# Sums of quarters kept in DRAM, and the last chunk of a down projection by seven products

## Chip, cores and metric

The kernel runs on one core of a Trainium2 chip. The metric is the device time of one execution in microseconds. The median of three runs of the kernel before is 2237.82 us (2236.54 to 2239.23).

## What is computed

Two decoder layers over 1024 tokens of width 1024. Layer 0 mixes tokens by a convolution module, layer 1 by sliding-window attention. In both, the mixer is followed by a layer norm, a squared-ReLU MLP with 4096 inner features, another layer norm, and a gated embedding. The change touches the MLP:

```python
def sq_relu_mlp(x, w_up, w_down):
    return jnp.square(jax.nn.relu(x @ w_up)) @ w_down
...
x = layer_norm(DEEPNORM_ALPHA * x + sq_relu_mlp(x, mlp_w_up[i], mlp_w_down[i]),
               mlp_ln_g[i], mlp_ln_b[i])
x = x + (p[i] @ ple_w_proj[i]) * jax.nn.sigmoid(x @ ple_w_gate[i])
```

## The kernel before

All matmuls are of float32 data, each operand split in a high part and a low part of the type fp32r. One product of a 128x128 block with a 128x512 block is three matmuls (`mm3`): high by high, high by low, low by high. Splitting is a cast on ScalarE (ACT) for the high part and a subtraction on VectorE (DVE) for the low one. A subtraction recorded for `nc.either` goes to DVE or to GpSimd (POOL).

The program is first recorded as a list of operations, each with a priority (its place in the list, plus an offset inside `later`). `Recorder.schedule` then runs through the list with a table of estimated costs and writes out a fixed order for each engine: at each moment it takes the ready operation with the lowest priority. Buffers are slots under tags ("t" has five, "z" four, "g" four, "wh" and "wl" five each, "raw" two, "zz" one, "bo" two), given out in the order of the requests and taken back when the last user ends. The eight PSUM banks are slots too, under "ps" and "tr" (transposes); `move` hands a slot from one tag to another. All DMAs are issued by SyncE, in one queue. Since a recorder writes every instruction, all of them carry one line in the profile (L433); tiles are told apart by their tag.

**Up products** (`mlp`). The 4096 inner features are 32 blocks of 128. The first four blocks in layer 0 (six in layer 1) and the last two are multiplied block by block (`up`: per block and half of the tokens, eight products over the width, 24 matmuls). The others go in pairs of blocks: a pair and the two halves of the tokens are a 2x2 problem, done with seven products of quarters (84 matmuls) instead of eight; sums of weight quarters (`pair_units`) and of token quarters (`token_forms`) are made on DVE. `square` applies relu and squares the result, and stores it at once in DRAM. `hid[i][c, j, h]` holds, for chunk c (four inner blocks), the blocks of parity j and the tokens of half h: a quarter of 128x1024, in two stores of 256 KB.

**Down products** (`down_seven`, `down_last`). The inner features are eight chunks of 512. A chunk is again a 2x2 problem: A is quarters of inner activations (half of the tokens by half of the chunk), B is quarters of `w_down`. `down_seven` does chunk 0 alone and chunks 1 to 6 two at a time (`DOWN`), by seven products. It loads quarters of A, and DVE makes the sums s1 to s4 of A and t1 to t4 of B. `form` splits each operand into tiles of xTh and xTl (eight of them in turn), and in the first chunk into tiles under `hid_tags`. `product` does the matmuls for four token tiles, into four banks, and `add_to` adds each bank to the residual tiles `self.x[t][q]` on DVE. Two groups of four banks are used: `one` for the products that share a1.b1, and `two`.

`down_last` does chunk 7 without sums: 8 products, run token tile by token tile, eight tiles of 24 matmuls. As soon as a token tile is complete, `layer_norm(t)` runs for it: statistics (DVE, with a power on POOL), scaling (ACT), gain (DVE), bias (`either`), then eight transposes on TensorE (PE) and their splits into xTh and xTl.

**The gate** (`ple`) follows at once: x @ w_gate for four token tiles at a time, first tiles 0 to 3, then 4 to 7, 24 matmuls a tile, from xTh and xTl. Its four weight units go through `prep` (load to "raw", cast on ACT, subtraction on `either`); in `down_last` the four units of `w_down` hold four of the five "wh" and "wl" slots until the last tile.

Of the kernel before, what the change touches and what calls it, by code (L numbers as in the profile page):

```python
# [15 lines left out]
P = 128  # L16
# [4 lines left out]
HT = 512  # L21
# [444 lines left out]
class Emit:  # L466
# [379 lines left out]
                    if cc == 1:  # L846
                        self.layer_norm(t, gb, self.mid[i])

    def square(self, i, f, h, src, tag="t"):
# [5 lines left out]
        nc.vector.scalar_tensor_tensor(out=sq, in0=src, scalar=0.0, in1=r, op0=ALU.max, op1=ALU.mult)  # L855
        o = f % 4 // 2 * HT
        nc.sync.dma_start(self.hid[i][f // 4, f % 2, h][:, o : o + HT], sq)

    def up(self, i, f, h, u):
# [5 lines left out]
        self.square(i, f, h, ps)  # L865

    def pair_units(self, i, f):

# [84 lines left out]
    def mlp(self, i):  # L953
# [9 lines left out]
        us = ws.get(4)  # L963
        for h in range(2):
            for f in first[:4]:
                self.up(i, f, h, us[f])
        ws.done(4)
        for f in first[4:]:
# [31 lines left out]
        for f in pairs:  # L1000
            w = ws.get(1)[0]
            p = prod(w, 0, plain[0, 0])
            c11 = copy(p)
            p2 = prod(w, 1, plain[1, 0])
            ws.done(1)
            w12 = ws.get(1)[0]
            prod(w12, 0, T[2], p)
            c21 = copy(p)
            self.square(i, f, 0, plus(c11, p2), "z")
# [5 lines left out]
            self.square(i, f + 1, 1, plus(c22, r), "z")  # L1015
            w = ws.get(1)[0]
            prod(w34, 1, plain[1, 1], p)
            self.square(i, f, 1, p, "z")
            prod(w, 0, T[4], r)
            ws.done(2)  # L1020
            self.square(i, f + 1, 0, plus(c21, r), "z")
        for f in last:
            u = ws.get(1)[0]
            for h in range(2):
                self.up(i, f, h, u)
            ws.done(1)

        self.x = []
        for t in range(NT):
# [3 lines left out]
        for k in range(3):  # L1033
            nc.move("tr", "ps")
        for n, cs in enumerate(DOWN):
            self.down_seven(i, cs, self.hid_tags if n == 0 else "")
        for k in range(3):
            nc.move("ps", "tr")
        gb = self.load_row("g", d["mlp_g"][i : i + 1]), self.load_row("g", d["mlp_b"][i : i + 1])
        self.down_last(i, NC - 1, gb)  # L1040

    def add_to(self, t, q, ps):

# [29 lines left out]
        self.nc.sync.dma_start(v, ap)  # L1073
        return v

    def down_seven(self, i, cs, tags):

        nc, d = self.nc, self.d
        sub, add = ALU.subtract, ALU.add
        n = len(cs)

        def A(tag, h, j):
            return [self.quarter(tag, self.hid[i][c, j, h]) for c in cs]

        def B(tag, j, q):
            return [self.quarter(tag, d["w_down"][i, c, j, q]) for c in cs]  # L1090

        def halves(tag, other):
            if tags:
# [12 lines left out]

        ftags = list(tags)

        def product(a, b, to, bank=None):
            f = [[self.form(v, ftags.pop(0) if ftags else None) for v in p] for p in zip(a, b)]  # L1110
# [15 lines left out]
        a11, b11 = A("wh", 0, 0), B("wl", 0, 0)  # L1126
        if tags:
            residual(0, 0)
        one = product(a11, b11, [(0, 0)])
        if tags:  # L1130
            m = [o for o in nc.ops if o.eng == "tensor"]
            residual(1, 1, m[-24 * n])
            residual(1, 0, m[-12 * n])
            residual(0, 1, m[-1])
        product(A("raw", 0, 1), B("wl", 1, 0), [(0, 0)])
        a21, b12 = A("wh", 1, 0), B("wl", 0, 1)
# [4 lines left out]
        s3 = tt(halves("z", 0), a11, a21, sub)  # L1141
        t3 = tt(halves("g", 1), b22, b12, sub)
        two = product(s3, t3, [(1, 1)])
        a22 = A("raw", 1, 1)
        s1 = tt(a21, a21, a22, add)
        s2 = tt(a11, s1, a11, sub)
# [4 lines left out]
        a12 = A("wh", 0, 1)  # L1151
        s4 = tt(a12, a12, s2, sub)
        product(s4, b22, [(0, 1)], one)
        a22, b21 = A("raw", 1, 1), B("wl", 1, 0)
        t4 = tt(b21, b21, t2, sub)
        product(a22, t4, [(1, 0)], two)

    def down_last(self, i, c, gb):

        nc, ws = self.nc, self.ws  # L1160
        ws.add(*[self.d["w_down"][i, c, j, q] for j in range(2) for q in range(2)])
        hid = {}
        for h in range(2):
            for j in range(2):
                for k in range(2):
                    raw = self.sb("t")
                    nc.sync.dma_start(raw, self.hid[i][c, j, h][:, k * HT : (k + 1) * HT])
                    hid[2 * k + j, h] = self.pair(self.hid_tags[h], F32R)
                    self.split(raw, *hid[2 * k + j, h])
        us = ws.get(4)  # L1170
        for t in range(NT):
            pss = [self.ps() for q in range(2)]
            o = t % 4 * P
            for b in range(4):
                hh, hl = hid[b, t // 4]
                for q in range(2):
                    wh, wl = us[b % 2 * 2 + q]
                    cs = slice(b // 2 * HT, (b // 2 + 1) * HT)
                    self.mm3(pss[q], [(hh[:, o : o + P], hl[:, o : o + P], wh[:, cs], wl[:, cs])], b == 0, b == 3)
            for q in range(2):  # L1180
                self.add_to(t, q, pss[q])
            self.layer_norm(t, gb)
        ws.done(4)

    def ple(self, i):
        nc, d, ws = self.nc, self.d, self.ws
# [40 lines left out]
    def attention(self):  # L1227
# [67 lines left out]
                    pend = p, n, gl, dict(vd), dst  # L1295
            ws.done(4)
        self.values(*pend)
        for a, b in (("ps", "sc"), ("ps", "sc"), ("ps", "pv")):
            nc.move(b, a)

        self.x = []
# [88 lines left out]
    def program(self):  # L1390
# [13 lines left out]
        for i in range(2):  # L1404
            for t in range(NT):
                nc.slots(f"mid{i}_{t}", [f"mid{i}_{t}"])
            for c in range(8):
                for k in range(4):
                    nc.slots(f"hid{i}_{c}_{k}", [f"hid{i}_{c}_{k}"])
        self.mid = [[nc.tile(f"mid{i}_{t}", (P, D), F32, "DRAM") for t in range(NT)] for i in range(2)]  # L1410
        self.hid = [
            {(c, k // 2, k % 2): nc.tile(f"hid{i}_{c}_{k}", (P, 1024), F32, "DRAM") for c in range(8) for k in range(4)}
            for i in range(2)
        ]
        self.ws = Stream(self)
# [103 lines left out]
```

## Time and profile before

| | |
|---|---|
| median of three runs | 2237.82 us |
| time of the profiled execution | 2238.38 us |
| its span | 2236.6 us |
| granted TensorE clock, mean | 0.998 |
| layer 0: first down chunk starts | 736.6 us |
| layer 0: last chunk of the down products | 1003.1 us |
| layer 0: gate products start | 1052.5 us |
| layer 1: waits of PE behind the last chunk | 2144.7 to 2155.1 us |

The profiled execution is one run of its own; its span runs from its first to its last instruction, and 1.8 us lie around it. "Busy" counts an instruction from start to end, and instructions of one engine overlap a little, so a sum of durations is more than the time they take one behind the other. PEld is the loading of weights into the array, which runs beside PE. A wait is put down to the engine that released it last.

### The profile page before, as it was taken

To read this page: it belongs to the slowest core of one execution; us is meant where nothing else is said; L and a number is where in the kernel's file an instruction comes from. 1 tells how busy PE (TensorE), PEld (TensorE's weight loads), DVE (VectorE), ACT (ScalarE), POOL (GpSimd) and SP (SyncE) were. 2 spreads that over 40 slices of the span, in tenths; PEclk is the share of its full clock that TensorE was granted. 3 is DMA by queue.
4 is the path that set the end of the run, shared out by engine and by line. 5 is a ranking of instruction groups with operands and counts; after the bars stand their busy time and mean duration, and the time that the engine had idled before them with its cause. 6 is when DMAs were issued, how large, how long until landed. Compare 5 with 4: busy or idle time off the path is not lost.

```text
span 2236.6 us, 28918 instructions
## 1 busy us (share of the span) xinstructions
PE 2196.3 (98%) x10412; PEld 1811.7 (81%) x10412; DVE 1601.4 (72%) x2596; ACT 927.1 (41%) x1709; POOL 361.2 (16%) x497
## 2 busy tenths in 40 slices
PE   8999999999999999999999999999999999999999
PEld 6888878788888888887778878777888888888877
DVE  6666586965555999978354888579565579889663
ACT  4333353544443333433245878333344433344231
POOL 2333362200000000005001555131000000000230
PEclk9999999999999999999999999999999999999999
DMA  7444642523336753530431011332333493444222
GB/s 222 109 111 98 170 132 82 194 85 113 113 113 199 254 168 127 170 118 19 132 99 38 21 38 39 106 106 81 103 110 113 119 318 129 158 160 132 66 85 99
DMA packets 128656, 271.38 MB, mean 121 GB/s; under 512 B 14081, under 2 KB 41857, under 8 KB 128513
## 3 DMA queue, kind: packets, MB, share of 16 engines
q1 hardware_dynamic: 128512, 269.54, 38.1%
q8 instruction: 82, 1.34, 0.3%
q14 instruction: 62, 0.50, 0.1%
HBM read 202.38 MB, written 67.11 MB: 120 GB/s over the span
## 4 chain that ended last, share of the span: by engine, by line
PE 87%; DVE 6%; POOL 2%; issue 1%; ACT 1%; DMA 1%; SPq 0%; POOLq 0%; DVEq 0%; ACTq 0%
PE ps L433 70%; PE tr L433 17%; DVE z L433 2%; DVE sm L433 1%; POOL sm L433 1%; DVE xTl L433 1%; DVE wl L433 1%; POOL B L433 1%; DVE E L433 1%; DMA raw<-in_w_in_dram 1%; ACT z L433 0%; DVE B L433 0%; DVE A L433 0%; SPq L433 0%; POOL wl L433 0%
## 5 line engine op out<-in xcount | busy, mean ns | idle before, releaser
L433 PE MATMUL ps<-xTh,wh 128*128 128x512 f32 x668 | 261.4, 394 | 4.7 <-ACT xTh L433 4.7
L433 PE MATMUL ps<-xTl,wh 128*128 128x512 f32 x668 | 263.1, 394 | 2.8 <-DVE xTl L433 2.8
L433 PE MATMUL ps<-xTh,wl 128*128 128x512 f32 x668 | 261.4, 391 | 0.0
L433 DVE TENSOR_TENSOR wl<-raw,wh 128x1024 fp32r<-128x1024 f32 (+2 forms) x130 | 145.8, 1124 | 133.2 <-ACT wh L433 132.2
L433 ACT CAST wh<-raw 128x1024 fp32r<-128x1024 f32 (+2 forms) x146 | 137.6, 943 | 230.7 <-PE ps L433 116.3
L433 PE MATMUL ps<-wh,xTh 128*128 128x512 f32 x572 | 230.2, 402 | 1.6 <-DVE xTh L433 1.5
L433 PE MATMUL ps<-wl,xTh 128*128 128x512 f32 x572 | 230.5, 403 | 0.0
L433 PE MATMUL ps<-wh,xTl 128*128 128x512 f32 x572 | 229.4, 402 | 0.1
L433 POOL TENSOR_TENSOR wl<-raw,wh 128x1024 fp32r<-128x1024 f32 x16 | 38.8, 2426 | 1138.0 <-ACT wh L433 1138.0
L433 PE MATMUL ps<-xTl,xTh 128*128 128x512 f32 x564 | 219.4, 389 | 0.0
L433 PE MATMUL ps<-xTh 128*128 128x512 f32 x564 | 219.4, 389 | 0.0
L433 PE MATMUL ps<-xTh,xTl 128*128 128x512 f32 x564 | 219.4, 389 | 0.0
L433 PEld LDWEIGHTS ps<-xTh,wh 128*128 128x128 f32 x668 | 125.9, 189 | 32.2 <-ACT xTh L433 5.0
L433 PEld LDWEIGHTS ps<-xTl,wh 128*128 128x128 f32 x668 | 125.9, 189 | 29.4 <-DVE xTl L433 4.8
L433 PEld LDWEIGHTS ps<-xTh,wl 128*128 128x128 f32 x668 | 126.0, 189 | 26.0
L433 DVE TENSOR_TENSOR wl<-g,wh 128x512 fp32r<-128x512 f32 x100 | 66.4, 686 | 110.0 <-ACT wh L433 110.0
L433 PEld LDWEIGHTS ps<-wh,xTh 128*128 128x128 f32 x572 | 108.0, 189 | 21.4 <-DVE xTh L433 1.8
L433 PEld LDWEIGHTS ps<-wh,xTl 128*128 128x128 f32 x572 | 107.8, 189 | 20.4 <-DVE xTl L433 0.3
L433 ACT CAST wh<-g 128x512 fp32r<-128x512 f32 x100 | 59.5, 620 | 155.9 <-PE ps L433 111.5
L433 PEld LDWEIGHTS ps<-wl,xTh 128*128 128x128 f32 x572 | 108.0, 189 | 19.6
L433 PEld LDWEIGHTS ps<-xTh,xTl 128*128 128x128 f32 x564 | 105.9, 188 | 22.1
L433 PEld LDWEIGHTS ps<-xTl,xTh 128*128 128x128 f32 x564 | 105.9, 188 | 21.9
(310 smaller groups left out, 5161.8 us busy)
## 6 DMA issues: line engine op xcount, KB each, us to landing
raw<-in_w_up_dram SPq DMA_DIRECT2D x64, 512.0 KB, 4.1
wl<-in_w_down_dram SPq DMA_DIRECT2D x56, 512.0 KB, 4.8
hid<-t SPq DMA_DIRECT2D x103, 256.0 KB, 2.0
raw<-hid SPq DMA_DIRECT2D x42, 512.0 KB, 4.0
wh<-hid SPq DMA_DIRECT2D x42, 512.0 KB, 5.2
scr<-zz SPq DMA_DIRECT2D x128, 64.0 KB, 2.1
B<-scr SPq DMA_DIRECT2D x32, 256.0 KB, 3.5
t<-proj SPq DMA_DIRECT2D x32, 256.0 KB, 3.6
```

Of the source, the lines that this page charges most:

```text
L433: getattr(getattr(nc, o.eng), o.name)(*a, **k)
```

## The change

- `square` no longer stores; it returns its tile. `keep` is called once per pair of inner blocks (also for pairs done by `up`), when all four quarters-of-a-pair c11, c12, c21, c22 are there. For chunk 0 it stores the four. For all other chunks it makes s1 to s4 with four DVE operations of 128x512 and stores seven tiles: s1 to s4 and three of the plain ones. The sums are held in "zz" (s1, s2), "bo" (s4) and in place (s3).
- `down_seven` makes s1 to s4 itself only in chunk 0. For the other chunks it loads them. The order of the seven products changes: all of bank group `one` first, then the two of group `two`.
- `down_last` is gone. Chunk 7 is done by `down_seven` with `end` set: after the fifth product (which completes token tiles 0 to 3) their layer norms are recorded with an offset of `LATE` = 100 in priority, and after the seventh product those of tiles 4 to 7. The last two products split their operands into tiles under `hid_tags`, so that xTh and xTl are free for the transposes.
- Around it: two "bo" slots, lent to the attention, are handed back.

```diff
+LATE = 100
...
-DOWN = (0,), (1, 2), (3, 4), (5, 6)
+DOWN = (0,), (1, 2), (3, 4), (5, 6), (7,)
...
+    def store(self, i, f, what, src):
         o = f % 4 // 2 * HT
-        nc.sync.dma_start(self.hid[i][f // 4, f % 2, h][:, o : o + HT], sq)
+        self.nc.sync.dma_start(self.hid[i][f // 4, what][:, o : o + HT], src)
+
+    def keep(self, i, f, c):
+
+        nc = self.nc
+        if f // 4 == 0:
+            for (j, h), v in c.items():
+                self.store(i, f + j, (j, h), v)
+            return
+        sub, add = ALU.subtract, ALU.add
+        w = nc.tile("zz", (P, 1024), F32)
+        s1, s2, s4 = w[:, 0:HT], w[:, HT : 2 * HT], self.sb("bo")
+        nc.vector.tensor_tensor(out=s1, in0=c[0, 1], in1=c[1, 1], op=add)
+        self.store(i, f, "s1", s1)
+        self.store(i, f, (1, 1), c[1, 1])
+        nc.vector.tensor_tensor(out=s2, in0=s1, in1=c[0, 0], op=sub)
+        self.store(i, f, "s2", s2)
+        s3 = c[0, 1]
+        nc.vector.tensor_tensor(out=s3, in0=c[0, 0], in1=s3, op=sub)
+        self.store(i, f, "s3", s3)
+        self.store(i, f, (0, 0), c[0, 0])
+        nc.vector.tensor_tensor(out=s4, in0=c[1, 0], in1=s2, op=sub)
+        self.store(i, f, "s4", s4)
+        self.store(i, f, (1, 0), c[1, 0])
...
+        def alone(f):
+            c = {}
+            for j in range(2):
+                u = ws.get(1)[0]
+                for h in range(2):
+                    c[j, h] = self.up(f + j, h, u)
+                ws.done(1)
+            self.keep(i, f, c)
+
+        for f in first[4::2]:
+            alone(f)
...
-            self.square(i, f + 1, 0, plus(c21, r), "z")
-        for f in last:
-            u = ws.get(1)[0]
-            for h in range(2):
-                self.up(i, f, h, u)
-            ws.done(1)
+            self.square(plus(c21, r), "z")
+            self.keep(i, f, {(0, 0): c11, (0, 1): c12, (1, 0): c21, (1, 1): c22})
+        for f in last[::2]:
+            alone(f)
...
         for n, cs in enumerate(DOWN):
-            self.down_seven(i, cs, self.hid_tags if n == 0 else "")
-        for k in range(3):
-            nc.move("ps", "tr")
-        gb = self.load_row("g", d["mlp_g"][i : i + 1]), self.load_row("g", d["mlp_b"][i : i + 1])
-        self.down_last(i, NC - 1, gb)
+            self.down_seven(i, cs, n == 0, n == len(DOWN) - 1)
...
+        def product(a, b, to, bank=None, own=False, last=False):
+            f = [[self.form(v, t if own else None) for v, t in zip(p, tags)] for p in zip(a, b)]
             new = bank is None
             bank = [self.ps() for t in range(4)] if new else bank
+            if last and to == [(0, 1)]:
+                for k in range(3):
+                    nc.move("ps", "tr")
...
+            for t in range(4 if last else 0):
+                with nc.later(LATE if to == [(0, 1)] else 0):
+                    self.layer_norm(t + 4 * to[0][0], gb)
             return bank
...
+        if start:
+            s3 = tt(halves("z", 0), a11, a21, sub)
+            s1 = tt(a21, a21, A("raw", (1, 1)), add)
+            s2 = tt(a11, s1, a11, sub)
+        else:
+            s2 = A("wh", "s2")
...
         product(s2, t2, [(1, 0)], one)
+        if not start:
+            s1 = A("wh", "s1")
         product(s1, t1, [(1, 1)], one)
...
+            s4 = A("wh", "s4")
+        if end:
+            gb = self.load_row("g", d["mlp_g"][i : i + 1]), self.load_row("g", d["mlp_b"][i : i + 1])
+        product(s4, b22, [(0, 1)], one, last=end)
+        if not start:
+            s3 = A("wh", "s3")
+        two = product(s3, t3, [(1, 1)], None, end)
+        a22, b21 = A("raw", (1, 1)), B("wl", 1, 0)
         t4 = tt(b21, b21, t2, sub)
-        product(a22, t4, [(1, 0)], two)
-
-    def down_last(self, i, c, gb):
...
+        product(a22, t4, [(1, 0)], two, end, end)
```

More of the change, by code (lines that the diff above doesn't have):

```diff
@@ L965, in mlp @@
             for f in first[:4]:
-                self.up(i, f, h, us[f])
+                self.store(i, f, (f % 2, h), self.up(f, h, us[f]))
         ws.done(4)
-        for f in first[4:]:
-            u = ws.get(1)[0]
-            for h in range(2):
-                self.up(i, f, h, u)
-            ws.done(1)
+        def alone(f):
[8 more added lines that the diff above has]
+            alone(f)
         T = self.token_forms(tags)
@@ L1074, in quarter, with down_seven @@
         return v
-    def down_seven(self, i, cs, tags):
+    def down_seven(self, i, cs, start, end):
         nc, d = self.nc, self.d
@@ L1084, in down_seven, with A @@
         n = len(cs)
-        def A(tag, h, j):
-            return [self.quarter(tag, self.hid[i][c, j, h]) for c in cs]
+        tags = self.hid_tags
+        def A(tag, what):
+            return [self.quarter(tag, self.hid[i][c, what]) for c in cs]
         def B(tag, j, q):
@@ L1124, in residual @@
                     nc.sync.dma_start(self.x[t][q], self.mid[i][t][:, q * HT : (q + 1) * HT])
-        a11, b11 = A("wh", 0, 0), B("wl", 0, 0)
-        if tags:
+        a11, b11 = A("wh", (0, 0)), B("wl", 0, 0)
+        if start:
             residual(0, 0)
-        one = product(a11, b11, [(0, 0)])
-        if tags:
+        one = product(a11, b11, [(0, 0)], own=start)
+        if start:
             m = [o for o in nc.ops if o.eng == "tensor"]
-            residual(1, 1, m[-24 * n])
-            residual(1, 0, m[-12 * n])
+            residual(1, 0, m[-24 * n])
+            residual(1, 1, m[-12 * n])
             residual(0, 1, m[-1])
-        product(A("raw", 0, 1), B("wl", 1, 0), [(0, 0)])
-        a21, b12 = A("wh", 1, 0), B("wl", 0, 1)
+        a12 = A("raw", (1, 0))
+        product(a12, B("wl", 1, 0), [(0, 0)])
+        a21 = A("wh", (0, 1)) if start else None
+        b12 = B("wl", 0, 1)
         b22 = halves("t", 1)
@@ L1140, in down_seven @@
                 nc.sync.dma_start(v[k], d["w_down"][i, c, 1, 1][:, k * HT : (k + 1) * HT])
-        s3 = tt(halves("z", 0), a11, a21, sub)
         t3 = tt(halves("g", 1), b22, b12, sub)
[L1143 to L1146, printed above, removed]
+        if start:
+            s3 = tt(halves("z", 0), a11, a21, sub)
[3 more added lines that the diff above has]
+            s2 = A("wh", "s2")
         t1 = tt(b11, b12, b11, sub)
@@ L1149, in down_seven @@
         product(s2, t2, [(1, 0)], one)
+        if not start:
+            s1 = A("wh", "s1")
         product(s1, t1, [(1, 1)], one)
[L1151 to L1154, printed above, removed]
-        t4 = tt(b21, b21, t2, sub)
-        product(a22, t4, [(1, 0)], two)
-    def down_last(self, i, c, gb):
[L1160 to L1183, printed above, removed]
+        if start:
+            a12 = A("wh", (1, 0))
+            s4 = tt(a12, a12, s2, sub)
+        else:
+            s4 = A("wh", "s4")
[6 more added lines that the diff above has]
+        a22, b21 = A("raw", (1, 1)), B("wl", 1, 0)
+        t4 = tt(b21, b21, t2, sub)
+        product(a22, t4, [(1, 0)], two, end, end)
     def ple(self, i):
@@ L1406, in program @@
                 nc.slots(f"mid{i}_{t}", [f"mid{i}_{t}"])
-            for c in range(8):
-                for k in range(4):
+            for c in range(NC):
+                for k in range(8):
                     nc.slots(f"hid{i}_{c}_{k}", [f"hid{i}_{c}_{k}"])
         self.mid = [[nc.tile(f"mid{i}_{t}", (P, D), F32, "DRAM") for t in range(NT)] for i in range(2)]
+        forms = [(0, 0), (0, 1), (1, 0), (1, 1), "s1", "s2", "s3", "s4"]
         self.hid = [
-            {(c, k // 2, k % 2): nc.tile(f"hid{i}_{c}_{k}", (P, 1024), F32, "DRAM") for c in range(8) for k in range(4)}
+            {
+                (c, v): nc.tile(f"hid{i}_{c}_{k}", (P, 1024), F32, "DRAM")
+                for c in range(NC) for k, v in enumerate(forms) if v in (forms[:4] if c == 0 else forms[:1] + forms[2:])
+            }
             for i in range(2)
```

23 lines of the change are left out of this document (8 added, 15 removed).

## The prediction

> **What bounds the kernel now.** I read the page first, for the share of each engine and the granted clock, then the chain that ended last for the spacing of matmuls, then the waits of PE in the stretches around the change.
>
> ```profile
> PE 2196.3 (98%) x10412; PEld 1811.7 (81%) x10412; DVE 1601.4 (72%) x2596; ACT 927.1 (41%) x1709; POOL 361.2 (16%) x497
> PEclk9999999999999999999999999999999999999999
> ```
> ```profile
> 472.90 35.36 PE ps L433 x156
> ```
>
> PE is busy for 98% of the span at full clock. In the chain, 156 matmuls on end take 35.36 us: 0.2267 us each. A matmul that goes away from a packed stretch is worth that much.
>
> The windows that follow are two stretches of up products in layer 0 (three pairs of inner blocks each), the first chunk of the down products, two double chunks, and the last chunk. Columns: window, length, then busy time of PE, PEld, DVE, ACT, POOL with instruction counts, granted clock, DMA share, GB/s.
>
> ```profile
> 560.00:617.10 57.10, 57.10 (x253) 47.26 (x252) 33.61 (x51) 23.38 (x40) 0.00 (x0) 1.00 0.36 111
> 617.10:674.20 57.10, 57.10 (x253) 47.25 (x252) 33.79 (x51) 23.38 (x40) 0.00 (x0) 1.00 0.36 111
> ```
> ```profile
> 736.60:774.70 38.10, 38.10 (x170) 31.56 (x169) 36.35 (x50) 12.92 (x16) 0.00 (x0) 1.00 0.71 264
> 774.70:850.80 76.10, 76.10 (x337) 63.04 (x336) 69.28 (x87) 27.50 (x34) 0.00 (x0) 1.00 0.44 145
> 850.80:927.00 76.20, 76.20 (x338) 63.10 (x337) 69.58 (x87) 29.46 (x38) 0.00 (x0) 1.00 0.47 159
> 1003.10:1046.60 43.50, 43.47 (x209) 34.79 (x208) 31.83 (x57) 12.31 (x19) 17.63 (x22) 1.00 0.02 9
> ```
>
> In all of these PE has no gap. VectorE (DVE) is 59% busy beside the up products and 91% beside the double chunks. Behind the last chunk, where the gate products begin, PE does wait: first layer 0 (from 1000 us), then layer 1 (from 2095 us); columns are total us, times, longest.
>
> ```profile
> PE ps L433 <- POOL B L433: 2.8, 3, 1.6
> ```
> ```profile
> PE tr L433 <- DVE xTl L433: 1.6, 1, 1.6
> PE ps L433 <- POOL B L433: 0.6, 1, 0.6
> PE tr L433 <- POOL B L433: 0.5, 1, 0.5
> ```
>
> So 2.8 us in layer 0 and 2.7 in layer 1: the normalised tokens come a little late for the gate.
>
> **The change part by part.** **The products.** The last chunk goes from 8 products (8 token tiles x 2 halves x 4 blocks x 3 = 192 matmuls) to 7 (7 x 4 tiles x 2 blocks x 3 = 168). That is 24 x 0.2267 = 5.44 us a layer, **10.88 us in all**. The code fixes this count. Whether it reaches the end depends on DVE, below.
>
> **The sums beside the up products.** Each pair of inner blocks outside chunk 0 gets four DVE operations of 128x512: 14 groups a layer, 28 in all. The trace has the same operation, and the form of 1024 that goes away, in the down stage (count, busy us, mean ns):
>
> ```profile
> L433 DVE TENSOR_TENSOR z<-wh,wh 128x512 f32<-128x512 f32 x8 | 5.1, 683 | 0.0
> L433 DVE TENSOR_TENSOR wh<-wh,wh 128x1024 f32<-128x1024 f32 x10 | 12.1, 1214 | 0.0
> L433 DVE TENSOR_TENSOR xTl<-wl,xTh 128x1024 fp32r<-128x1024 f32 x26 | 31.6, 1216 | 0.0
> L433 DVE TENSOR_TENSOR B<-B,ps 128x512 f32<-128x512 f32 x34 | 23.0, 679 | 1.3 <-PE ps L433 1.3
> ```
>
> 4 x 0.683 = 2.73 us a pair. A pair is 84 matmuls = 19.04 us, so DVE goes from 33.7 to 33.7 + 3 x 2.73 = 41.9 of 57.1 us, 73%. Cost taken: nothing, since idle DVE time hides it. Without that cover it would be up to 28 x 2.73 = 76 us; a gain is excluded, because PE has no gap there. I take the zero end because of who waits for whom between 560 and 680 us:
>
> ```profile
> ACT wh L433 <- PE ps L433: 41.8, 16, 4.6
> ```
> ```profile
> SPq L433 <- DVE t L433: 73.3, 13, 7.6
> ```
>
> The weight casts wait for PE to give a weight buffer back, so weights are ready ahead of need. SyncE's queue already stands behind stores that wait for DVE, up to 7.6 us, and PE does not notice. A pair now issues seven stores, not four; behind a late one stand the next weight loads, for which the casts wait. Inner tiles are held until the last sum (three of five "t" slots, one of four "z"), so the next pair's first two copies still find a slot.
>
> **The down chunks.** For chunks 1 to 6, DVE loses 2 x 0.683 + 3 x 1.214 = 5.0 us a chunk: a double chunk falls from 69.3 to 59.3 of 76.1 us. PE has no gap to close there: gain nothing. The order changes (the second bank group last), but a bank's add still has the time of three other token tiles before that bank is written again (4.1 us in a single chunk, against 0.68 for an add).
>
> **Transfers.** Stores grow by 3 quarters (0.524 MB) in each of 14 chunks, loads by 10 quarters a layer: 32.5 MB more.
>
> ```profile
> q1 hardware_dynamic: 128512, 269.54, 38.1%
> hid<-t SPq DMA_DIRECT2D x103, 256.0 KB, 2.0
> ```
>
> At the same rate the queue goes from 38.1% to about 43%. The dense place is the first chunk (share 0.71 above), and it loads no sums. Cost nothing; an estimate for the other end is one exposed 2.0 us landing per layer, 4 us.
>
> **DVE in the last chunk.** Five products with two forms each, 10 x 1.216; two with forms in halves, 8 x 0.683; weight sums 3 x 1.214 + 2 x 0.683; 28 adds x 0.679: 41.6 us, against 38.1 us of PE. Rows overlap when DVE runs without a gap: the next rows start 0.59 apart though each lasts 0.67.
>
> ```profile
> 1034.24 0.67 DVE L433 TENSOR_TENSOR B<-B,ps 128x512 f32<-128x512 f32 x1
> 1034.83 0.68 DVE L433 TENSOR_TENSOR z<-z,g 128x512 f32<-128x512 f32 x1
> ```
>
> By starts the 41.6 become some 37.5, and the chunk ahead now leaves DVE 17 us idle to prepare the first forms. Cost nothing; other end 41.6 - 38.1 = 3.5 us a layer.
>
> **The normalisation.** Now each token tile is finished every 5.44 us, and its normalisation overlaps the next tile. Afterwards tiles 0 to 3 finish with the fifth product, tiles 4 to 7 with the seventh. Call E the end of the fifth product: the gate can start at E + 10.9, and by tiles needs one more every 5.44 us. DVE's share, from 1003 to 1075 us, for eight tiles:
>
> ```profile
> L433 DVE TENSOR_TENSOR z<-z,g 128x512 f32<-128x512 f32 x16 | 14.3, 907 | 2.9 <-ACT z L433 2.9
> L433 DVE TENSOR_TENSOR xTl<-ps,xTh 128x512 fp32r<-128x512 f32 x11 | 7.5, 680 | 4.4 <-ACT xTh L433 4.4
> L433 DVE BATCH_NORM_STATS2 sm<-B 128x6 f32<-128x512 f32 x8 | 5.4, 682 | 0.0
> L433 DVE BATCH_NORM_STATS2 sm<-E 128x6 f32<-128x512 f32 x8 | 5.1, 677 | 0.0
> L433 DVE TENSOR_TENSOR wl<-raw,wh 128x1024 fp32r<-128x1024 f32 x2 | 4.5, 2243 | 0.3 <-ACT wh L433 0.3
> L433 DVE SCALAR_TENSOR_TENSOR sm<-sm,sm 128x1 f32<-128x1 f32 x8 | 3.5, 432 | 6.3 <-POOL sm L433 6.3
> L433 DVE TENSOR_TENSOR xTl<-tr,xTh 128x512 fp32r<-128x512 f32 x5 | 3.4, 670 | 0.0
> L433 DVE BATCH_NORM_AGGREGATE sm<-sm 128x2 f32<-128x12 f32 x8 | 1.6, 206 | 0.2
> ```
> ```profile
> 1009.38 1.28 DVE L433 BATCH_NORM_STATS2 sm<-E 128x6 f32<-128x512 f32 x2
> 1023.27 0.68 DVE L433 TENSOR_TENSOR xTl<-tr,xTh 128x512 fp32r<-128x512 f32 x1
> 1058.72 1.27 DVE L433 BATCH_NORM_STATS2 sm<-B 128x6 f32<-128x512 f32 x2
> ```
>
> Without the weight splits (4.5) these are 40.8 / 8 = 5.1 us a tile. The first tile takes 14.6 us from its statistics to its last piece (1023.95 - 1009.38); the tiles follow each other at (1058.72 - 1009.38) / 7 = 7.05 us. That pace holds 5.1 of normalisation, 2 x 0.68 of adds, 0.6 of gate-weight splits: 7.0, partly overlapped, with idle time between.
>
> Afterwards the adds left behind E - 4 are 12 for eight tiles (1.0 us a tile), and the gate weights can be split earlier, since the last chunk gives its buffers back product by product: 6.1 us a tile by durations, 5.4 by starts. Tile 0 has its statistics at E - 3.5 and is ready at E + 11.1, where the gate starts at E + 10.9. At 5.4 us a tile PE waits 0.2 us; at 6.1 the wait is 0.2 + 7 x (6.1 - 5.44) = 4.8 us; the middle is 2.5, about the 2.8 of now. I take **no change** here; bounds from -2.8 to +8.7 us a layer, the last from the pace of now (rival 1).
>
> One rule can be held against this. DVE's multiply takes twice its time while POOL adds:
>
> ```profile
> 1028.58 1.40 DVE L433 TENSOR_TENSOR z<-z,g 128x512 f32<-128x512 f32 x1
> ```
> ```profile
> 1028.14 1.29 POOL L433 TENSOR_TENSOR E<-z,g 128x512 f32<-128x512 f32 x1 [1.85 <-DVE z L433]
> ```
>
> 1.40 against 0.68 above. The Trainium skill, "SBUF — State Buffer", section "Who interferes with whom", says that a DVE instruction with two SBUF inputs contends with a GpSimd instruction that reads SBUF, and the later one waits. By it all four new sums would wait if POOL worked beside them; the windows of up products show POOL at 0.00, so by this rule the sums keep their 0.68, and it bites only at the normalisation, where its price is already in the 0.907 of the first row.
>
> **Sum.** 2238.38 us (the profiled execution; its span is 2236.6) - 10.88 = 2227.5. That execution was 0.56 above the median of 2237.82, so the forecast is **2227 us**, 0.5% faster.
>
> **The rivals.** **1, slower: the normalisation in two bursts.** If DVE keeps the pace of 7.05 us a tile, the last tile makes PE wait 0.2 + 7 x (7.05 - 5.44) = 11.5 us a layer, 8.7 more than now, against the 5.44 saved: 2 x 3.3 = 6.5 over the median, 2244. It decides from a pace of 5.44 + (2.8 + 5.44 - 0.2) / 7 = 6.6 us a tile. For it: DVE's order is fixed and it idles between dependent steps. Against: four tiles at once give it something to do in those gaps.
>
> **2, the saved products stand behind DVE.** The chunk takes DVE's 41.6 us instead of 38.1; the change does not do what it says: 43.5 - 41.6 = 1.9 saved a layer, 2234. For: single chunks have the least DVE room (36.35 of 38.10 in the first). Against: PE had no gap even there, and the overlap of rows.
>
> **3, the up products stall.** A wait of 0.4 us in each of 28 groups (a held "t" slot, a store ahead of a weight load) gives 11 us, 2238. Against: the casts' wait above; for: seven stores in one queue.
>
> **4, the gate stalls vanish,** since its weights are split earlier: 5.5 less, 2221.5.
>
> **How the numbers follow.** Forecast 60% (2222 to 2232, stalls 2.5 us a layer either way); rival 1 12%, its pace anywhere between 6.4 and 7.2 (2235 to 2246); rival 2 8%; rival 3 10% (2230 to 2250); rival 4 10% (2219 to 2223). Range 2221 to 2241: half of rival 4 and most of the far halves of 1 and 3 lie outside, some 17%. A measurement can tell about 0.2%, 4.5 us. Faster: 58 from the forecast, 10 from 4, 3 from 2: 71%. Slower: 7 from 1, 4 from 3: 11%. The same: 18%.
>
> **What would show it.** PE's count falls by 48. Windows of up products: PE still packed, DVE near 73%, POOL at zero. Double chunks: DVE near 59 of 76 us. The last chunk takes 38 us; behind it PE waits 0 to 5 us a layer. Wrong would be: PE waits on DVE inside the last chunk (2), between up products (3), or over 8 us for xTh and xTl at the gate (1).

## The result, and the profile after

The changed kernel takes **2249.28 us** (2248.63 to 2249.85) where the kernel before takes 2237.49 on the same chip: a ratio of 1.0052, 95% interval 1.0034 to 1.0069. It is 0.5% slower; the forecast was 0.5% faster. The profiled execution has a span of 2247.8 us against 2236.6, so 11.2 us have to be found.

The page of the kernel after: the engines, one group of its costliest, and the DMA queue.

```profile
PE 2195.7 (98%) x10364; PEld 1802.1 (80%) x10364; DVE 1679.8 (75%) x2673; ACT 937.7 (42%) x1711; POOL 422.5 (19%) x510
...
q1 hardware_dynamic: 142624, 302.05, 41.5%
...
L434 POOL TENSOR_TENSOR wl<-raw,wh 128x1024 fp32r<-128x1024 f32 x43 | 113.3, 2637 | 1094.3 <-ACT wh L434 653.3
```

PE has its 48 matmuls less (10412 to 10364), and the queue is at 41.5%. What nobody asked for is in the last line: 43 low parts of weights are now split on POOL. Before they were 16, of 2426 ns each. (All lines are L434 now, since the recorder's line has moved by one.)

**Where the time went.** The same matmuls of both kernels, put side by side in their timelines, give this (us from the start):

| | before | after | later by |
|---|---|---|---|
| layer 0: second product of chunk 0 | 742.02 | 748.32 | 6.30 |
| layer 0: a matmul behind the last chunk and the gate | 1200.54 | 1206.25 | 5.71 |
| layer 1: a transpose that waits for DVE in both, ahead of the up products | 1511.32 | 1515.56 | 4.24 |
| layer 1: second product of chunk 0 | 1827.93 | 1838.38 | 10.45 |
| end | 2236.6 | 2247.8 | 11.2 |

The up stages lose 6.3 and 10.45 - 4.24 = 6.2 us, 12.5 together. From the down products on, the kernel gains 2.06 us in layer 0 (up to the transpose) and loses 0.75 more in layer 1 (up to the end). The seven products save 5.44 there, so 3.4 and 6.2 come back as something else. Sum: 12.5 - 10.9 + 9.6 = 11.2. In layer 0 it is in fact 4.9 that come back by 1200 us (only 0.59 of the 5.44 are left); 1.5 us are gained later, in the attention, where the kernel before had a slow clock (at the end of the next part).

**Beside the up products.** The windows of the kernel after; the third is a stretch of double chunks, for comparison (columns as in the prediction):

```profile
540.00:600.00 60.00, 59.09 (x258) 47.89 (x257) 44.10 (x62) 24.73 (x42) 8.21 (x3) 1.00 0.44 148
600.00:660.00 60.00, 59.11 (x258) 47.90 (x258) 43.85 (x62) 23.83 (x41) 8.73 (x3) 1.00 0.44 146
836.60:896.60 60.00, 60.00 (x267) 49.67 (x266) 50.03 (x60) 20.97 (x24) 0.00 (x0) 1.00 0.57 184
```

DVE is at 73% as forecast, but POOL is not at zero, and PE is not packed: 258 matmuls in 60 us, where a packed stretch has 266 or 267. One pair of blocks shows why. First POOL, then DVE, ACT and PE in the timeline of the kernel after (start, length, what; in brackets idle time before and who ended it):

```profile
547.90 2.39 POOL L434 TENSOR_TENSOR wl<-raw,wh 128x1024 fp32r<-128x1024 f32 x1 [17.31 <-PE ps L434]
```
```profile
547.33 0.68 DVE L434 TENSOR_TENSOR t<-t,ps 128x512 f32<-128x512 f32 x1
547.93 2.92 DVE L434 TENSOR_TENSOR z<-t,z 128x512 f32<-128x512 f32 x1
550.77 0.68 DVE L434 TENSOR_TENSOR g<-raw 128x512 f32<-128x512 f32 x1
...
554.38 0.67 DVE L434 TENSOR_TENSOR t<-t,ps 128x512 f32<-128x512 f32 x1
```
```profile
555.15 0.63 ACT L434 ACTIVATE z<-t 128x512 f32<-128x512 f32 x1 [1.84 <-DVE t L434]
555.69 0.56 ACT L434 COPY t<-ps 128x512 f32<-128x512 f32 x1
```
```profile
555.60 0.39 PE L434 MATMUL tr<-E,wl 128*128 128x512 f32 x1
556.31 0.74 PE L434 MATMUL ps<-A,wh 128*128 128x512 f32 x2 [0.32 <-ACT t L434]
```

Read it from the top. POOL subtracts a weight unit from 547.90 to 550.29. In those 2.4 us DVE stands in one new sum (the s3 of `keep`): 2.92 us for what takes 0.69 elsewhere. DVE has no gap from there to 555.1 us (the window, same columns),

```profile
550.90:555.10 4.20, 4.20 (x20) 3.50 (x19) 4.20 (x8) 1.25 (x2) 0.00 (x0) 1.00 0.50 187
```

so the lost 2.2 us stay with it: the addition at 554.38 is late, with it the relu on ACT, behind that the copy that empties a bank, and PE has nothing to do at about 556. The pair costs 19.64 us instead of 19.04, seen in a cast on ACT that comes once a pair:

```profile
559.17 1.14 ACT L434 CAST wh<-g 128x512 fp32r<-128x512 f32 x2 [2.92 <-PE ps L434]
578.81 1.14 ACT L434 CAST wh<-g 128x512 fp32r<-128x512 f32 x2 [2.88 <-PE ps L434]
```

POOL's timeline shows the split in 11 of the 13 pairs of layer 0 and in 10 of the 12 of layer 1; 21 pairs at 0.60 make 12.6 us, against the 12.5 of the table. It is not always the same operation that is held up: in the pairs that follow, s3 begins just ahead of POOL (587.26 and 587.29) and keeps its 0.69 us, and a sum of weights (`g<-raw`, from 588.41) takes 2.35 us instead, with the same loss a pair. The view of waits puts only 3.4 us on it between 480 and 720 us, because the rest lies in matmuls that are shown longer around each wait (two in 0.74 instead of 0.62): the count in the window is the safer reading.

**Behind the last chunk.** The waits of PE in the kernel after, from 1000 us (layer 0), then from 2080 us (layer 1):

```profile
PE ps L434 <- DVE B L434: 3.4, 1, 3.4
PE ps L434 <- DVE xTl L434: 1.6, 3, 0.9
PE ps L434 <- POOL E L434: 0.5, 2, 0.3
```
```profile
PE ps L434 <- DVE B L434: 3.7, 1, 3.7
PE tr L434 <- DVE xTl L434: 0.9, 1, 0.9
PE ps L434 <- DVE xTl L434: 0.7, 2, 0.4
PE tr L434 <- POOL A L434: 0.3, 1, 0.3
PE ps L434 <- POOL A L434: 0.2, 1, 0.2
```

The waits for the normalised tokens (xTl, E, A) have become smaller than before: 2.1 us a layer, against 2.8 and 2.7. The 3.4 and 3.7 are new, and they are inside the last chunk: the last product needs a bank whose add (B) DVE has not done. DVE and POOL just before, in the same timeline:

```profile
1016.62 2.88 DVE L434 TENSOR_TENSOR xTl<-wh,xTh 128x1024 fp32r<-128x1024 f32 x1
...
1020.03 1.21 DVE L434 TENSOR_TENSOR xTl<-wl,xTh 128x1024 fp32r<-128x1024 f32 x1
...
1022.36 2.59 DVE L434 TENSOR_TENSOR xTl<-wh,xTh 128x1024 fp32r<-128x1024 f32 x1
...
1028.48 0.66 DVE L434 TENSOR_TENSOR B<-B,ps 128x512 f32<-128x512 f32 x1
```
```profile
1016.02 2.41 POOL L434 TENSOR_TENSOR wl<-raw,wh 128x1024 fp32r<-128x1024 f32 x1 [6.26 <-ACT wh L434]
1021.47 2.40 POOL L434 TENSOR_TENSOR wl<-raw,wh 128x1024 fp32r<-128x1024 f32 x1 [3.04 <-DVE xTl L434]
```

It is the same meeting of POOL and DVE: splits of the gate's weights on POOL, and the forms of the last chunk at 2.88 and 2.59 us instead of 1.21, with DVE full. A stretch of windows shows a second price (same columns):

```profile
1025.60:1029.30 3.70, 0.34 (x3) 0.04 (x1) 3.70 (x7) 0.44 (x1) 0.00 (x0) 1.00 0.48 175
1029.30:1033.20 3.90, 3.90 (x10) 3.11 (x11) 3.90 (x7) 0.00 (x0) 0.00 (x0) 0.56 0.01 4
1033.20:1037.00 3.80, 3.80 (x18) 3.13 (x17) 2.98 (x6) 0.00 (x0) 2.40 (x1) 1.00 0.00 0
```

After the gap the granted clock is 0.56 for 3.9 us, and 10 matmuls are done where the next 3.8 us hold 18. At 0.2267 us 3.9 us would hold 17, so the gap costs 7 x 0.2267 = 1.6 us more than its own length. With 3.4 + 1.6, less 0.7 of the smaller waits, layer 0 should lose 4.3 here; 4.9 came back, and the other 0.6 was not placed. In layer 1 the low clock lasts longer:

```profile
2119.70:2123.60 3.90, 3.88 (x9) 3.13 (x10) 3.90 (x7) 0.00 (x0) 0.31 (x1) 0.50 0.04 15
2123.60:2127.60 4.00, 4.00 (x15) 3.14 (x14) 2.72 (x5) 0.00 (x0) 2.07 (x1) 0.78 0.24 37
```

That is 24 matmuls in 7.9 us where 35 would fit, 11 x 0.2267 = 2.5 us. With the gap of 3.7, less 0.6 of the smaller waits, this makes 5.6 of the 6.2; again 0.6 was not placed.

The Trainium skill, "TensorE: Matmul & The Clock Gate", Part 1, section "What's actually happening", has a rule for it: idle for a window of about 3.4 us, the array is put back to half its rate, until it has been busy for about as long. The 0.56 and 0.50 behind the gaps agree. But the trace also has a case that the rule in these words does not cover. In the attention, the kernel before has this (same columns):

```profile
1408.20:1411.60 3.40, 1.77 (x10) 1.13 (x9) 3.26 (x14) 1.81 (x7) 0.00 (x0) 1.00 0.67 226
1411.60:1415.20 3.60, 3.59 (x9) 2.83 (x10) 2.49 (x9) 2.93 (x13) 1.73 (x4) 0.53 0.74 217
```

PE was busy for half of the 3.4 us, with waits of 1.2 us at most, and yet the clock fell; 9 matmuls where 16 would fit cost 1.6 us. In the kernel after the same work (1.77 of 3.4 us busy, from 1414.0) left the clock at 1.00: these are the 1.5 us gained there, and the change did not earn them. The wait of 1.6 us at the gate of the kernel before left it at 1.00 too. Which gaps below 3.4 us cost clock is not shown here.

### The profile page after: what moved, and what is told of

It is laid out like the page before. It is cut to its first block, busy times and chain, and to the rows that moved or that the text cites. A ratio compares the mean times of both kernels' runs of the same rounds, so it can differ in the third digit from the quotient of the medians.

```text
span 2247.8 us, 29231 instructions
## 1 busy us (share of the span) xinstructions
PE 2195.7 (98%) x10364; PEld 1802.1 (80%) x10364; DVE 1679.8 (75%) x2673; ACT 937.7 (42%) x1711; POOL 422.5 (19%) x510
## 3 DMA queue, kind: packets, MB, share of 16 engines
q1 hardware_dynamic: 142624, 302.05, 41.5%
## 4 chain that ended last, share of the span: by engine, by line
PE 73%; DVE 15%; issue 5%; DMA 3%; ACT 2%; POOL 1%; SPq 0%; DVEq 0%; ACTq 0%; POOLq 0%
PE ps L434 57%; PE tr L434 15%; DVE wl L434 3%; DVE z L434 3%; DVE xTl L434 3%; DMA raw<-in_w_up_dram 2%; DVE sm L434 1%; DVE t L434 1%; DVE B L434 1%; DVE E L434 1%; ACT wh L434 1%; DVE A L434 1%; DVE g L434 1%; DVE bo L434 1%; ACT t L434 1%
## 5 line engine op out<-in xcount | busy, mean ns | idle before, releaser
L434 POOL TENSOR_TENSOR wl<-raw,wh 128x1024 fp32r<-128x1024 f32 x43 | 113.3, 2637 | 1094.3 <-ACT wh L434 653.3
L434 PE MATMUL ps<-xTh,wh 128*128 128x512 f32 x660 | 258.3, 394 | 5.6 <-ACT xTh L434 5.6
L434 PE MATMUL ps<-xTl,wh 128*128 128x512 f32 x660 | 259.9, 394 | 1.7 <-DVE xTl L434 1.7
L434 PE MATMUL ps<-xTh,wl 128*128 128x512 f32 x660 | 258.5, 392 | 0.0
L434 PE MATMUL ps<-xTh 128*128 128x512 f32 x636 | 249.0, 392 | 7.1 <-DVE B L434 7.1
L434 PE MATMUL ps<-xTh,xTl 128*128 128x512 f32 x636 | 248.9, 391 | 0.0
L434 PE MATMUL ps<-xTl,xTh 128*128 128x512 f32 x636 | 248.8, 391 | 0.0
L434 ACT CAST wh<-raw 128x1024 fp32r<-128x1024 f32 (+2 forms) x138 | 129.4, 938 | 219.1 <-PE ps L434 113.9
L434 PE MATMUL ps<-wh,xTh 128*128 128x512 f32 x468 | 188.8, 404 | 1.5 <-DVE xTh L434 1.4
L434 PE MATMUL ps<-wl,xTh 128*128 128x512 f32 x468 | 189.9, 406 | 0.0
L434 PE MATMUL ps<-wh,xTl 128*128 128x512 f32 x468 | 188.7, 405 | 0.9 <-DVE xTl L434 0.8
L434 DVE TENSOR_TENSOR wl<-raw,wh 128x1024 fp32r<-128x1024 f32 (+2 forms) x95 | 98.9, 1044 | 112.3 <-ACT wh L434 111.6
L434 PEld LDWEIGHTS ps<-xTh,wh 128*128 128x128 f32 x660 | 124.4, 189 | 32.6 <-ACT xTh L434 5.6
L434 PEld LDWEIGHTS ps<-xTh 128*128 128x128 f32 x636 | 120.2, 189 | 32.9 <-issue 7.9
L434 PEld LDWEIGHTS ps<-xTl,wh 128*128 128x128 f32 x660 | 124.4, 188 | 27.4 <-DVE xTl L434 3.2
L434 PEld LDWEIGHTS ps<-xTh,wl 128*128 128x128 f32 x660 | 124.3, 188 | 25.9
L434 PEld LDWEIGHTS ps<-xTh,xTl 128*128 128x128 f32 x636 | 120.1, 189 | 25.3
L434 PEld LDWEIGHTS ps<-xTl,xTh 128*128 128x128 f32 x636 | 120.2, 189 | 24.8
L434 ACT CAST xTh<-wh 128x1024 fp32r<-128x1024 f32 x74 | 77.6, 1049 | 122.5 <-PE ps L434 93.4
L434 DVE TENSOR_TENSOR wl<-g,wh 128x512 fp32r<-128x512 f32 x100 | 64.6, 684 | 73.3 <-ACT wh L434 73.3
L434 ACT CAST wh<-g 128x512 fp32r<-128x512 f32 x100 | 59.5, 620 | 140.7 <-DVE g L434 66.3
L434 POOL TENSOR_TENSOR E<-cst,g 128x1152 fp32r<-128x1152 f32 x32 | 78.8, 2465 | 145.9 <-PE ps L434 141.5
```

What stands on the lines that cost most here:

```text
L434: getattr(getattr(nc, o.eng), o.name)(*a, **k)
```

## The experiments

The theory after this reading: **(1)** the change makes DVE busier; the planner, which has a free choice for subtractions marked `either`, moves some to POOL; POOL's reading holds DVE up, and DVE has no slack left to absorb it. Rivals: **(2)** seven stores a pair in SyncE's queue, or the held "t" slots, delay the up products; **(3)** the four sums themselves are too much for DVE; **(4)** the weights split on POOL are simply ready too late. All medians stand beside runs of the kernel before on the same chip; ratios are to those.

**1. The up stage's split back on DVE.** From the kernel after, in `pair_units`:

```diff
-            nc.either.tensor_tensor(out=wl, in0=raw[0], in1=wh.bitcast(F32), op=ALU.subtract)
+            nc.vector.tensor_tensor(out=wl, in0=raw[0], in1=wh.bitcast(F32), op=ALU.subtract)
```

> The kernel after, with one word changed: the split of the first weight unit of each pair goes to DVE always, never to POOL. Theory 1 (POOL's read of SBUF holds up DVE operations with two SBUF inputs, the late squares make PE wait some 0.6 us a pair): POOL at 0.0 beside the up products, no 2.4 to 2.9 us DVE operations there, a pair at 19.04 us again, both layers together 13 to 15 us faster than after: 2234 to 2237 us. Theory 2 (the four sums and their stores themselves hold up the squares, by DVE's order or by held slots): DVE gets still more work, pairs stay at 19.6 us or more, 2249 us or more.

Measured: 2238.67 us (2234.75 to 2240.91), ratio 0.9996 (0.9987 to 1.0006): one operation per pair on another engine gives back the whole loss of 0.5%. (The median is a little above the 2234 to 2237 of theory 1. Side by side with the kernel after, the same matmuls gain 6.60 us over the up stage of layer 0 and 6.10 over that of layer 1: what the two stages had lost.) One of its windows, and from 540 to 660 us the groups of the sum s3 and of the weight sum (busy us, mean ns, idle before); then the same groups in the kernel after:

```profile
560.00:617.10 57.10, 57.10 (x254) 47.06 (x253) 40.80 (x64) 23.41 (x39) 0.00 (x0) 1.00 0.43 152
```
```profile
L434 DVE TENSOR_TENSOR z<-t,z 128x512 f32<-128x512 f32 x6 | 4.1, 685 | 0.0
L434 DVE TENSOR_TENSOR g<-raw 128x512 f32<-128x512 f32 x6 | 4.1, 683 | 0.0
```
```profile
L434 DVE TENSOR_TENSOR z<-t,z 128x512 f32<-128x512 f32 x6 | 6.3, 1058 | 0.0
L434 DVE TENSOR_TENSOR g<-raw 128x512 f32<-128x512 f32 x6 | 12.6, 2105 | 2.1 <-DMA raw<-in_w_up_dram 2.1
```

In the kernel after, s3 was held up in one of these six pairs and the weight sum in the other five; the 2.1 us for which DVE waited there for a weight load are gone in experiment 1, with the same stores in the queue. PE is packed, with every sum and every store still there: rivals 2 and 3 fall. This is the window that the prediction had described. The stall in the last chunk is still there (3.3 and 3.7 us).

**2. The gate's splits on DVE too.** On top of experiment 1, `prep` uses DVE while `ple` (the gate) runs:

```diff
-        nc.either.tensor_tensor(out=wl, in0=raw, in1=wh.bitcast(F32), op=ALU.subtract)
+        (nc.vector if self.pin else nc.either).tensor_tensor(out=wl, in0=raw, in1=wh.bitcast(F32), op=ALU.subtract)
```

> As e1, and also the splits of the gate weights go to DVE always (LN's bias adds stay free to go to POOL). If the stall of 3.5 to 3.9 us near the end of the last chunk, and the 4 us of slower clock behind it, come from POOL's splits blocking DVE there, both are gone: about 5 us a layer, 2224 to 2228 us, faster than before. If they come from DVE's load in the last chunk alone, they stay: as e1, 2234 to 2239 us.

Measured: 2230.3 us (2229.6 to 2232.22), ratio 0.9966 (0.9953 to 0.9978), above the 2224 to 2228 that was expected. The wait of 3.4 us and the low clock behind it are gone; the waits for the gate's tokens have grown in place of it. Its waits of PE from 1045 to 1140 us, the same row as from 2130 to 2200:

```profile
PE ps L434 <- DVE xTl L434: 3.3, 3, 1.3
```

**3 and 4. POOL reads, POOL writes.** Is it the sharing of reads, or rival 4, a late weight? Both kernels take experiment 1, where the weights are split on DVE, and add useless work on POOL to each pair, into a spare tile that nobody reads. Experiment 3 reads SBUF:

```diff
+            v = self.sb("v")
+            for c in (L, R):
+                nc.gpsimd.tensor_tensor(out=v, in0=raw[0][:, c], in1=wh.bitcast(F32)[:, c], op=ALU.subtract)
```

> e1 plus useless work: in each pair POOL does two subtractions of 128x512 from the same raw weights into a spare tile that nobody reads. The weights themselves still come from DVE, so nothing waits for POOL's result. If it is the sharing of reads, DVE operations of 1.4 to 3 us and the waits of PE come back, 6 to 15 us over e1. If it was the lateness of weights split on POOL (2.4 us instead of 1.2), it stays at e1's time.

Experiment 4 only writes (the copy of one column sets the place in time):

```diff
+            v = self.sb("v")
+            nc.scalar.copy(v[:, 0:1], wh.bitcast(F32)[:, 0:1])
+            for k in range(4):
+                nc.gpsimd.memset(v, 0.0)
```

> e1 plus useless work that only writes: POOL does four memsets of 128x512 into the spare tile per pair, behind a copy of one column on ACT. If only a GpSimd instruction that reads SBUF holds up DVE, this stays within 2 us of e1; if any POOL work on SBUF does, it is slower like e3.

Measured: 2247.39 us with reads, 2235.76 with writes (one run each; the kernel before there 2236.11 to 2241.06). One window of each (reads, then writes), and the groups on POOL and of s3 from 540 to 660 us (again reads, then writes):

```profile
560.00:617.10 57.10, 56.65 (x247) 45.75 (x246) 47.18 (x63) 22.46 (x38) 11.98 (x6) 1.00 0.42 149
```
```profile
560.00:617.10 57.10, 57.10 (x254) 47.22 (x253) 40.99 (x63) 23.67 (x42) 6.33 (x12) 1.00 0.43 153
```
```profile
L434 POOL TENSOR_TENSOR v<-raw,wh 128x512 f32<-128x512 f32 x12 | 24.0, 1996 | 93.0 <-ACT wh L434 92.5
...
L434 DVE TENSOR_TENSOR z<-t,z 128x512 f32<-128x512 f32 x6 | 10.6, 1774 | 0.0
```
```profile
L434 POOL MEMSET v<- 128x512 f32 x24 | 12.7, 527 | 101.6 <-ACT v L434 100.6
...
L434 DVE TENSOR_TENSOR z<-t,z 128x512 f32<-128x512 f32 x6 | 4.1, 686 | 0.0
```

Reads that nobody uses bring the loss back: 247 matmuls for 254, s3 at 1774 ns. Writes do nothing. (The 2235.76 is 2.9 us under the median of experiment 1, and within its runs.) The loss needs no late weight, and in the kernel after no wait of PE in the up stages is put down to one: rival 4 falls too. The rule that the prediction quoted from the Trainium skill, "SBUF — State Buffer", section "Who interferes with whom", holds here on both sides: it names the GpSimd instruction that reads SBUF and leaves out the one that only writes, and only the first held DVE up.

**5. The sums alone.** Experiment 1 with the last chunk by eight products again (`down_last` restored, chunk 7 stored plain):

```diff
-DOWN = (0,), (1, 2), (3, 4), (5, 6), (7,)
+DOWN = (0,), (1, 2), (3, 4), (5, 6)
...
-        if f // 4 == 0:
+        if f // 4 in (0, NC - 1):
```

> The kept sums alone, with the up split on DVE as in e1: chunks 1 to 6 load their sums, chunk 7 is done as before the change (eight products, layer norm tile by tile, gate splits free as before). My theory: sums that do not meet POOL cost nothing and bring nothing, since PE was packed in both stages: 2236 to 2240 us, as before. If the sums cost something of their own (stores, slots, DVE's order): over 2242 us.

Measured: 2239.18 us (2238.34 to 2240.77), ratio 1.0005 (0.9996 to 1.0015), up windows packed, and at the gate the waits of the kernel before (2.8 in layer 0, 2.8 in layer 1). The sums by themselves neither cost nor bring anything.

**6. The last chunk alone.** Experiment 2 with plain quarters stored everywhere, so that each chunk makes its own sums:

```diff
-        if f // 4 == 0:
+        if True:
...
-        if start:
+        if True:
             s3 = tt(halves("z", 0), a11, a21, sub)
```

> The seven products of chunk 7 alone, with up and gate splits on DVE as in e2: nothing but the four plain quarters is stored, and every chunk makes its sums in the down stage as before the change. If the kept sums only move work off a place where PE was packed, this is as fast as e2, 2228 to 2232 us. If the last chunk needs DVE's time (4.6 us of sums come back there, 46 against 38 us of PE), PE waits 3 to 8 us a layer more: 2236 to 2246 us.

Measured: 2247.97 us (2245.32 to 2249.16), ratio 1.0040 (1.0025 to 1.0055), just above the range that was given. Its window over the last chunk has DVE busy without a gap:

```profile
1003.00:1045.00 42.00, 42.00 (x193) 33.87 (x191) 42.00 (x68) 13.56 (x19) 8.77 (x12) 1.00 0.10 32
```

The seven products fit, but what DVE does not get done there it does at the gate, where PE waits 4.6 us for xTl and 3.8 for others in layer 0. The last chunk by seven products therefore needs the kept sums: experiment 2 has them, and its ratio is 0.9966 against 1.0040. (Part of that is again the clock, with a mean of 0.994 in the profiled execution here and 0.999 there.)

**7, 8, 10. The rest of the gate's waits.** Three edits on top of experiment 2: the bias of the second layer norm always on POOL, `LATE` = 0, `LATE` = 200.

```diff
-            nc.either.tensor_tensor(out=xt[q], in0=z, in1=gb[1][q], op=ALU.add)
+            (nc.gpsimd if spill is None else nc.either).tensor_tensor(out=xt[q], in0=z, in1=gb[1][q], op=ALU.add)
```
```diff
-LATE = 100
+LATE = 0
```
```diff
-LATE = 100
+LATE = 200
```

> e2 with the bias adds of the MLP's layer norm always on POOL (in e2 five of sixteen go to DVE and take 1.2 to 1.4 us there). If the rest of the waits at the gate (3.3 us a layer) is DVE's load, it falls by 1 to 3 us a layer: 2225 to 2229 us. If it is the mutual blocking, POOL's longer use blocks DVE's multiplies more: 2230 us or more.

> e2 with LATE = 0: the layer norms of tiles 0 to 3 come ahead of the forms and adds of the last two products. If these norms are what the gate waits for, 1 to 3 us a layer less: 2225 to 2229 us; if the last two products then wait for their forms or adds, more: 2231 to 2238 us.

> e2 with LATE = 200, so that tiles 0 to 3 are normalised behind the last two products' work. If the offset matters little, 2228 to 2233 us like e2 and e8; if the gate's first tiles come late, 2235 us or more.

Measured: 2231.34 us (ratio 0.9968, 0.9956 to 0.9981) with the bias on POOL; 2234.77 (0.9985, 0.9975 to 0.9994) with `LATE` = 0; 2239.66 (1.0008, 0.9999 to 1.0018) with `LATE` = 200. Each came out in the slower of its two expected ranges, and none is faster than experiment 2. The waits move with the order: at `LATE` = 0 they fall on the adds B (1.5 and 1.2 us) and on xTl (1.9), at 200 on one late xTl, in the waits of PE from 980 to 1140 us:

```profile
PE tr L434 <- DVE xTl L434: 4.3, 1, 4.3
PE ps L434 <- POOL E L434: 1.1, 1, 1.1
PE tr L434 <- ACT xTh L434: 0.5, 1, 0.5
```

**9. The kernel before with only the gate's splits on DVE** (the edit of experiment 2, nothing of the change):

> The kernel before, with only the splits of the gate weights put on DVE always. It shows how much of e2's gain is the pin itself. If POOL's splits among the layer norms cost the kernel before its 2.8 us of waits a layer: 2232 to 2235 us. If the gain of e2 over before is the saved products: 2236 to 2239 us, no change.

Measured: 2232.12 us (2231.14 to 2234.23), ratio 0.9975 (0.9965 to 0.9986). Its only wait at the gate in layer 0, from 980 to 1140 us:

```profile
PE ps L433 <- DVE B L433: 0.4, 1, 0.4
```

So most of the gain of experiment 2 over the kernel before needs none of the change. Whether the change adds anything on top, the times leave open (ratios 0.9966 and 0.9975, with intervals that overlap). The two traces say a little more. Ahead of layer 0's last chunk a matmul of experiment 2 is 0.80 us later than the same one of experiment 9 (987.00 against 986.20), and among the gate's products 0.09 earlier (1080.98 against 1081.07); in layer 1 the lead grows from 0.99 (2061.97 against 2062.96) to 1.95 (2174.47 against 2176.42). That is 0.9 and 1.0 us, of 5.44 saved in each. Most of the rest goes to the waits at the gate: 3.6 us in layer 0 against 0.4, and 3.3 against 0.4 in layer 1.

**11. The kernel before with the up stage's split on POOL.** The meeting without the sums:

```diff
-            nc.either.tensor_tensor(out=wl, in0=raw[0], in1=wh.bitcast(F32), op=ALU.subtract)
+            nc.gpsimd.tensor_tensor(out=wl, in0=raw[0], in1=wh.bitcast(F32), op=ALU.subtract)
```

> The kernel before, without any sums beside the up products, with the split of the first weight unit of each pair put on POOL always. If the blocking of DVE alone makes PE wait, this loses 6 to 16 us: 2244 to 2254 us. If DVE's idle time (41% there) takes the blocking up as long as the sums are absent, it stays within 3 us of before.

Measured: 2238.9 us (2237.81 to 2240.54), ratio 1.0004 (0.9994 to 1.0013): nothing. Yet DVE is held up, as its groups from 540 to 660 us show, and POOL's:

```profile
L433 DVE SCALAR_TENSOR_TENSOR t<-t,z 128x512 f32<-128x512 f32 x19 | 23.9, 1258 | 9.4 <-ACT z L433 9.4
```
```profile
L433 POOL TENSOR_TENSOR wl<-raw,wh 128x1024 fp32r<-128x1024 f32 x6 | 14.4, 2394 | 99.9 <-PE ps L433 99.9
```

The same operation has 688 ns in experiment 1. DVE is idle for 38% of the up stage here (busy for 35.62 us in each window of 57.10), and that idle time takes the delay up: PE is packed in both windows. So the four combinations are: neither 1, POOL's split alone 1.0004, the sums alone 0.9996 to 1.0005 (experiments 1 and 5), both 1.0052 (the kernel after and experiment 1 have the last chunk by seven products too).

## Why the prediction was wrong

- **The products**, -5.44 a layer: right. PE's count falls by 48.
- **The sums beside the up products: the first step that failed.** It read "Cost taken: nothing, since idle DVE time hides it"; the up stages lost 12.5 us. The sums by themselves are hidden, with DVE at 71% in experiment 1 (73% forecast; experiment 5 agrees). But the step priced them as if everything else stayed on its engine. The kernel before has a planner and a subtraction that is free to go to POOL, both of which stand in the description; with 2.73 us more a pair on DVE, the subtraction of one weight unit went there in 21 of 25 pairs (that the planner's estimate of DVE's load was the reason is argued from the code; that it went is in the trace). The prediction then even wrote down the rule that made this costly, and put it aside with "the windows of up products show POOL at 0.00". That row was true of the kernel before and was taken as a property of the stage.
- **The last chunk: the second step that failed.** For DVE in the last chunk the prediction took "Cost nothing; other end 41.6 - 38.1 = 3.5 us a layer", and for the normalisation "no change". The sum of both was 4.9 us in layer 0 and 6.2 in layer 1, where the forecast took zero. "The gate weights can be split earlier" was true; they were split inside the last chunk, on POOL, where DVE is full, and the price was a wait for an add (3.4 and 3.7 us) and a low clock behind it (1.6 and 2.5 us), which no term of the sum had. With the splits on DVE (experiment 2) that wait is gone, so DVE's 41.6 us alone did not cause it, and the waits at the gate are 3.3 to 3.6 us a layer, by 0.6 to 0.8 above those of before. That is close to "no change", but against experiment 9, which has the same splits on DVE, it is 3 us a layer more.
- **Rival 3** had the place and nearly the size: 0.4 us in each of 28 groups, 11 us, against 0.60 in 21 pairs, 12.6 us. Its mechanisms, a held "t" slot or stores ahead of weight loads, are not what happened, since both are still there in experiment 1; and its time of 2238 us had no part for the last chunk. That the measured 2249.28 lies inside its range (2230 to 2250) is luck.
- **The other rivals.** The 11.5 us of waits a layer that rival 1 gave for the gate were 2.1 in the kernel after; rival 4 (no waits) was not seen either; rival 2's place is where the add was late, from another cause.
- **The down chunks and the transfers**: no wait of PE came from either. DVE is busy for 61.3 and 59.7 us in two stretches of 76.1 (59.3 forecast), and the queue is at 41.5% (estimated 43).
- **The sum.** 2238.4 - 10.9 + 12.5 + 9.6 = 2249.6, the time of the profiled execution. The two last terms are read off the timelines, so the sum is a check of the bookkeeping; of the 9.6, 0.6 us a layer has no cause shown, and without the low clock in the attention of the kernel before it would be 1.5 more.

## What to carry to other kernels

Before work is added to an engine, look for the operations that a planner may then place elsewhere, and price the change with them moved as well: a row that shows an engine idle is a fact of that schedule, not of the stage. A contention that costs nothing while the engine has 38% idle time (experiment 11) can cost the whole gain and more when it has 27% (the kernel after), so neither the contention nor the added work is to be priced alone. And if the best kernel of a series owes its gain to an edit that would also help the kernel before, run that edit there too.

## What was not expected of the hardware

- A DVE operation of 128x512 on two SBUF operands that meets a POOL subtraction ends about its own time after that one: 2.92 us beside one of 2.39 that began just ahead of it, 2.35 beside one of 2.91 that had begun 1.1 us before, in both 0.56 us after POOL's end, where it has 0.68 alone. POOL's memsets of 527 ns, 24 of them in the same 120 us, leave it at 686 ns.
- It is mutual: the subtraction on POOL has 2394 to 2426 ns in the kernels with an emptier DVE and a mean of 2637 in the kernel after, the longest of those looked at 3.43 us.
- A gap of 3.4 us on PE was followed by 3.9 us at a granted clock of 0.56, which adds about half of the gap once more (1.6 us), and one of 3.7 us by 3.9 us at 0.50 and 4.0 at 0.78 (2.5 us). Once the clock fell to half behind 3.4 us in which PE was busy for 1.77; in another kernel the same stretch left it at 1.00.
